# Tracing the RWKV branch's bonus sum behind the DeltaNet branch's second projection, and down's first split two steps earlier

## Chip, core and metric

One core of a Trainium2 chip runs the whole layer as one program. The metric is the device time of one execution in microseconds (us), the median of several runs. The engines are called by their names and by those in the profile: TensorE (PE; its weight loads are PEld), Vector (DVE), Scalar (ACT), GpSimd (POOL), and SyncE (SP), whose queue issues nearly all transfers.

## The reference, cut to what matters

A decoder layer on 1040 tokens (16 meta tokens and 1024) of width 1024, all in float32: a half-step SwiGLU network, a mixer of two branches A and B, a second SwiGLU network.

```python
h = h + 0.5 * swiglu(rmsnorm(h, g1), w_gu1, w_down1)     # hidden width 2816
u = rmsnorm(h, gm)
aq, ak, av, az, abeta, aalpha, bcols, ga, gb = split(u @ w_in)
# A: causal conv of 4 taps on q, k, v, then silu; q, k to unit length; chunked gated DeltaNet
# B: r, k, v from bcols (token shift); RWKV-7 scan gives y, group norm, then
y = y + sum(r * k * r_k, axis=head) * v                  # the bonus
h = h + (sigmoid(ga) * o_a + sigmoid(gb) * o_b) @ w_out
h = h + 0.5 * swiglu(rmsnorm(h, g2), w_gu2, w_down2)
out = rmsnorm(h, gf)[meta tokens dropped]
```

## The kernel before, in words

**Precision.** Every large product is made of parts in a fast matmul format. `split` (L155) writes a rounded copy `hi` with Scalar and the remainder `lo` with Vector; for weights and activations in `mm3` (L255) each 128-row step takes three matmuls: weights hi by input hi, weights hi by input lo, weights lo by input hi. So the third matmul of a projection is the first to read the weights' remainder.

**The networks.** `ffn1` and `ffn2` compute gate and up products in units (`gate_up`, L435), store the hidden tiles to DRAM, and `down` (L606) loads them back, splits each (`Hidden.put`, L577) and multiplies. A generator `Hidden.ahead` (L582) is stepped inside the last two units of `gate_up`: its first step issues the loads of the first three hidden tiles, later steps fetch and split two weight tiles, and one step splits hidden tile 0 into a tile of its own (`hd0`).

**The mixer.** `middle` (L802) runs 16 iterations: 8 pairs of heads for a first token segment of 528 columns (16 meta and 512), then the same 8 for the second segment of 512. The order of the parts within an iteration is written out in strings (L183 to L188); the regular one is "merge_blocks transitions operands+ inverses+ chains gates finish decay++ new_b++ new_a++", where each + is an iteration ahead. Two parts matter here, always one after the other:

- `new_b` (L1138) projects B's v, k and r for the iteration two ahead (`shifted` calls `proj`, which is 24 matmuls of 512 columns in the second segment, 48 of half that width in the first), normalizes k into kkn with a column sum over TensorE (`colsum_rsqrt`, L1041), and forms the inputs of the scan on Vector. Its last lines (L1181 to L1186) are the bonus: Vector makes bv = r * r_k * k, Scalar and Vector split it into the pair `hl`, TensorE sums it over each head's 64 rows with two matmuls into the bank `bon`, and Vector multiplies by v. The product is read by `finish` (L1640) two iterations later.
- `new_a` (L1189) does A's k, q and v in this order: projection, evacuation by Scalar into xr and acc, three taps of the conv on Vector (L1209), a silu on Scalar, and for k and q a column sum for the length (`cs`, `ones`).

`hl` is one pair for all column sums (`parts_tile`, L1035, one buffer). v, k, r, kkn, xr and acc are tiles of the tag `tmp`, eight slots, each of which is handed on when its last reader is done.

**What sets the order of the work.** The code only traces the instructions. When the kernel is built, a planner that works with its own costs for each instruction fills each engine's queue: of the instructions that it takes to be ready, the one traced earliest goes first; one traced later may go ahead while an earlier one isn't ready. The queues so made are fixed, and on the chip each engine takes its own in that order. In the trace, `bon`'s two matmuls have others between and around them that were traced later. Moving code in the trace order thus moves a rank, not a place.

**Weights.** `loadw` (L228) keeps one weight tile fetched ahead: when a projection is traced, the next one's transfer and split are traced with it. Two buffers hold the split weights.

Of the kernel before, what the change touches and what calls it, by code (L numbers as in the profile page):

```python
# [9 lines left out]
F32R = mybir.dt.float32r  # L10
AF = mybir.ActivationFunctionType
ALU = mybir.AluOpType
# [14 lines left out]
FULL = 512  # L27
# [127 lines left out]
def split(g, src, hi, lo, eng=None, hi_eng=None):  # L155
    if hi_eng:
        hi_eng.tensor_copy(hi, src)
    else:
        g.nc.scalar.activation(hi, src, AF.Copy)  # L159
    (eng or g.nc.vector).tensor_tensor(lo, src, hi.bitcast(F32), op=ALU.subtract)  # L160
# [55 lines left out]
def fetchw(g):  # L216
    if not g.worder[g.wfetched]:
        del g.worder[g.wfetched]
    name, idx, kk = g.worder[g.wfetched]
    g.wfetched += 1  # L220
    raw = g.wp.tile([P, KD, P], F32, name="wraw", tag="wraw", bufs=2)
    g.nc.sync.dma_start(raw[:, :kk, :], g.a[name][idx])
    w = g.wp.tile([P, 2, KD, P], F32R, name="w", tag="w", bufs=WB)
    split(g, raw[:, :kk, :], w[:, 0, :kk, :], w[:, 1, :kk, :])
    g.wready.append((name, idx, w))


def loadw(g, name, *idx):  # L228

    while g.wfetched < min(g.wused + 1 + AHEAD, len(g.worder)) and g.worder[g.wfetched]:  # L230
        fetchw(g)
    g.wused += 1
    n, i, w = g.wready.pop(0)
    assert (n, i) == (name, idx)
    return w
# [12 lines left out]
def mm_tile(g, name, n=512, first=256):  # L248

    t = g.mm.tile([P, 512 * g.mmw], F32, name=name, tag="mm")  # L250
    o = 512 - first if n > 512 else 0
    return t[:, o : o + n]


def mm3(g, ps, w, kk, rhs):  # L255
    n = 3 * kk
    i = 0
    for k in range(kk):
        hi, lo = rhs(k)
        for l, r in ((w[:, 0, k, :], hi), (w[:, 0, k, :], lo), (w[:, 1, k, :], hi)):  # L260
            g.nc.tensor.matmul(ps, lhsT=l, rhs=r, start=i == 0, stop=i == n - 1)  # L261
            i += 1
# [298 lines left out]
class Hidden:  # L561
# [20 lines left out]
    def ahead(self):  # L582
        for f in range(self.AHEAD):
            self.load(f)
        yield
        yield
        fetchw(self.g)
        yield
        self.first = self.put(self.tile(self.pool, F32R, "hd0", "hd0", 1, [2]))
        yield  # L590
        yield
        fetchw(self.g)
        yield
# [274 lines left out]
def tmp_tile(g, name, w=528):  # L868
    return g.st.tile([P, w], F32, name=name, tag="tmp", bufs=NTMP)
# [54 lines left out]
def proj(g, c, ct, full=False):  # L924

    w = loadw(g, "win", ct)
    lo, n = (c.off, FULL) if full else (0, c.n)
    ps = mm_tile(g, "pp", n, FULL // 2 + c.off)
    for c0, cn in halves(n, FULL // 2 + c.off):
        sl = slice(lo + c0, lo + c0 + cn)  # L930
        mm3(g, ps[:, c0 : c0 + cn], w, KD, lambda k: (c.u[k][:, 0, sl], c.u[k][:, 1, sl]))
    return ps
# [92 lines left out]
def halves(n, first=256):  # L1025
    return [(0, first), (first, n - first)] if n > 512 else [(0, n)]
# [111 lines left out]
def new_b(g, q):  # L1138

    nc, st, V, c, j, n, off, it = g.nc, g.st, g.V, q.c, q.j, q.n, q.off, q.it  # L1140
    meta = q.s == 0
    fs = slice(off, off + FULL)
    tmp = lambda name, w=528: tmp_tile(g, name, w)
    EN, ELx, av, elm = q.EN, q.ELx, q.av, meta and q.elm

    v = shifted(g, c, 48 + j, 16 + j, "vB")


    Vs = q.Vs = st.tile([P, NCB, CB], F32, name="Vs", tag="Vs", bufs=2)
    k = shifted(g, c, 40 + j, 8 + j, "kB")  # L1150
    for ps, cs in run(g, g.mx, "vbp", lambda i, h: (v[HS[h], off + i * CB : off + (i + 1) * CB],
                                                    g.C("cmat")[HS[h], HS[h]], h, key(i, h)))[0]:
        nc.scalar.activation(Vs[:, cs], ps, AF.Copy)
    if meta:
        ps = g.mx.tile([P, 512], F32, name="vbm", tag="mx")
        nc.tensor.matmul(ps[:16, 0:P], lhsT=v[:, 0:16], rhs=g.C("cmat"), start=True, stop=True)
        nc.scalar.activation(g.uvm[it % 2][0:16, :], ps[:16, 0:P], AF.Copy)

    r = shifted(g, c, 32 + j, j, "rB")
    kkn = tmp("kkn")  # L1160
    colsum_rsqrt(g, "bd", k[:, :n], kkn, kkn, n, 1.0, V("eps"), pre=V("kk", j))
    nc.vector.scalar_tensor_tensor(kkn[:, :n], k[:, :n], V("kk", j), kkn[:, :n], op0=ALU.mult, op1=ALU.mult)
    t1 = tmp("t1")
    nc.vector.tensor_tensor(t1[:, :n], av[:, :n], kkn[:, :n], op=ALU.mult)
    nc.scalar.activation(av[:, :n], av[:, :n], AF.Identity, scale=V("ka", j), bias=V("oka", j))
    nc.vector.tensor_tensor(k[:, :n], k[:, :n], av[:, :n], op=ALU.mult)
    BK = q.BK = st.tile([P, NCB, 2, CB], F32, name="BK", tag="BK")
    nc.vector.tensor_tensor(BK[:, :, 1, :], ch3(k[:, fs], CB), ch3(EN[:, fs], CB), op=ALU.mult)
    nc.vector.scalar_tensor_tensor(BK[:, :, 0, :], ch3(t1[:, fs], CB), -1.0, ch3(EN[:, fs], CB),
                                   op0=ALU.mult, op1=ALU.mult)  # L1170
    AR = q.AR = st.tile([P, NCB, 2, CB], F32, name="AR", tag="AR", bufs=2)
    nc.vector.tensor_tensor(AR[:, :, 0, :], ch3(kkn[:, fs], CB), ELx[:, :, 0:CB], op=ALU.mult)
    if meta:
        arm = q.arm = st.tile([P, 16], F32, name="arm", tag="arm", bufs=2)
        nc.vector.tensor_tensor(arm, kkn[:, 0:16], elm[:, 0:16], op=ALU.mult)
        nc.vector.tensor_tensor(g.bkm[:, 0:16], k[:, 0:16], EN[:, 0:16], op=ALU.mult)
        nc.vector.scalar_tensor_tensor(g.bkm[:, 32:48], t1[:, 0:16], -1.0, EN[:, 0:16], op0=ALU.mult, op1=ALU.mult)

    nc.vector.tensor_tensor(AR[:, :, 1, :], ch3(r[:, fs], CB), ELx[:, :, 1:], op=ALU.mult)
    bv = q.bv = st.tile([P, FULL], F32, name="bv", tag="bv", bufs=2)  # L1180
    nc.vector.scalar_tensor_tensor(bv, r[:, fs], V("rk", j), k[:, fs], op0=ALU.mult, op1=ALU.mult)  # L1181
    ps = g.mx.tile([P, 512], F32, name="bon", tag="mx")
    hi, lo = parts_tile(g, FULL)
    split(g, bv, hi, lo)
    colsum(g, ps, "bd", hi, lo)
    nc.vector.tensor_tensor(bv, ps, v[:, fs], op=ALU.mult)  # L1186


def new_a(g, q):  # L1189

    nc, st, V, c, j, n, off = g.nc, g.st, g.V, q.c, q.j, q.n, q.off
    meta = q.s == 0
    tmp = lambda name, w=528: tmp_tile(g, name, w)
    kq = q.kq = st.tile([P, 2, 528], F32, name="kq", tag="kq", bufs=2)
    for wi, base in ((0, 8), (1, 0), (2, 16)):
        ct = base + j
        ps = proj(g, c, ct)
        xr = tmp("xr", 531)
        acc = tmp("acc")
        if c.s == 0:  # L1200
            nc.gpsimd.memset(xr[:, 0:3], 0.0)
        else:
            nc.gpsimd.tensor_copy(xr[:, 0:3], g.carA[:, ct, :])
        nc.scalar.activation(xr[:, 3 : 3 + n], ps, AF.Copy)
        nc.scalar.activation(acc[:, :n], ps, AF.Identity, scale=V("convw", ct * 4 + 3))  # L1205
        if c.s == 0:
            nc.gpsimd.tensor_copy(g.carA[:, ct, :], xr[:, n : n + 3])
        for tap in (2, 1, 0):
            nc.vector.scalar_tensor_tensor(acc[:, :n], xr[:, tap : tap + n], V("convw", ct * 4 + tap), acc[:, :n],  # L1209
                                           op0=ALU.mult, op1=ALU.add)  # L1210
        sg = xr
        sigm(nc, sg[:, :n], acc[:, :n], scale=-1.0)
        nc.vector.tensor_tensor(acc[:, :n], acc[:, :n], sg[:, :n], op=ALU.mult)
        if wi < 2:
            colsum_rsqrt(g, "ones", acc[:, :n], sg, sg, n, 1.0, V("eps"),
                         bias=V("lnq") if wi == 1 else None)
            nc.vector.tensor_tensor(kq[:, wi, :n], acc[:, :n], sg[:, :n], op=ALU.mult)
    Va = q.Va = st.tile([P, NCA, P], F32, name="Va", tag="Va", bufs=2)
    ps = g.mx.tile([P, 512], F32, name="vap", tag="mx")
    for i in range(NCA):  # L1220
        nc.tensor.transpose(ps[:, i * P : (i + 1) * P], acc[:, off + i * CA : off + (i + 1) * CA], g.C("ident"))
    nc.scalar.activation(Va, ch3(ps, P), AF.Copy)
    if meta:
        vkm = q.vkm = st.tile([16, 2, P], F32, name="vkm", tag="vkm", bufs=2)
        ps = g.mx.tile([P, 512], F32, name="vmp", tag="mx")
        nc.tensor.matmul(ps[:16, 0:P], lhsT=acc[:, 0:16], rhs=g.C("ident"), start=True, stop=True)
        nc.scalar.activation(vkm[:, 0, :], ps[:16, 0:P], AF.Copy)
# [510 lines left out]
```

## Time and profile before

| | |
|---|---|
| median of 3 runs | 3052.4 us (3052.31 to 3053.04) |
| the profiled execution | 3048.16 us |
| its span, first to last instruction | 3046.4 us |
| TensorE busy | 2942.3 us, 97% |
| Vector busy | 2007.7 us, 66% |
| Scalar busy | 1372.2 us, 45% |
| GpSimd busy | 348.6 us, 11% |
| mean granted clock of TensorE, share of full | 0.993 |

The span is that of the one execution whose trace was taken; its own time is 1.8 us longer, and the median of the runs 4.2 us above that. A timeline row reads: start, duration, engine, source line, operation, output <- inputs by tile names, shape, count of merged instructions, and in brackets the idle time of that engine just before, with what released it. The first network runs to about 732 us; the last column sum of the mixer is at 2301.7 us, and the second network follows the output projection, from 2364 us on.

### The profile page before, as it was taken

What the parts mean: (1) busy time and instruction counts of PE and PEld (TensorE: products, weight loads), DVE (VectorE), ACT (ScalarE), POOL (GpSimd) and SP (SyncE); (2) the same over time, 40 slices, a digit from 0 to 9 for tenths busy, and PEclk for the clock granted to TensorE, in tenths of its full rate; (3) what the DMA queues carried; (4) which work ended last, traced back from release to release, by engine and by line L of the source; (5) the groups of instructions that cost most, each with busy time, mean ns of one, the idle gap of its engine ahead of it and who ended that gap; (6) DMA issues with size and microseconds to landing.
All of it is one profiled execution on the core that took longest, in us unless ns stands there. A gap on an engine that the chain in (4) does not pass through costs nothing.

```text
span 3046.4 us, 61663 instructions
## 1 busy us (share of the span) xinstructions
PE 2942.3 (97%) x25498; PEld 2530.1 (83%) x25498; DVE 2007.7 (66%) x3872; ACT 1372.2 (45%) x2404; POOL 348.6 (11%) x503
## 2 busy tenths in 40 slices
PE   8999999999989999999998999999999999999998
PEld 8999998998878888888776777777786888888886
DVE  7555554346668877778868888777766755556246
ACT  5322222125645656556565655665544432223114
POOL 0322220000000000000000110010000032232000
PEclk9999999999999999999999999999999999999999
DMA  3232224234222322233332333223345132225223
GB/s 127 83 98 84 83 82 160 81 94 149 80 67 72 78 74 67 78 82 97 82 92 67 91 80 81 74 74 88 106 145 178 64 104 90 83 83 202 58 80 115
DMA packets 257593, 287.19 MB, mean 94 GB/s; under 512 B 169296, under 2 KB 175440, under 8 KB 257312
## 3 DMA queue, kind: packets, MB, share of 16 engines
q1 hardware_dynamic: 253072, 271.43, 30.2%
q0 software_dynamic: 2512, 8.65, 0.8%
q8 instruction: 201, 3.29, 0.5%
q10 hardware_dynamic: 1728, 3.16, 0.3%
q14 instruction: 80, 0.66, 0.1%
HBM read 232.70 MB, written 50.47 MB: 93 GB/s over the span
## 4 chain that ended last, share of the span: by engine, by line
PE 52%; DVE 10%; ACT 5%; issue 2%; DMA 1%; SPq 0%; DVEq 0%; ACTq 0%
PE pp L261 16%; PE pg L448 13%; PE pd L261 8%; PE pwo L261 3%; PE pg L472 1%; DVE w L160 1%; DVE tb L1400 1%; DVE Xb L1402 1%; ACT w L159 1%; PE vp L1085 1%; PE cs L1032 1%; PE mp L1085 1%; PE np L1085 1%; DVE mt L1508 1%; PE bkt L1317 1%
## 5 line engine op out<-in xcount | busy, mean ns | idle before, releaser
L261 PE MATMUL pp<-uk,w 128*128 128x512 f32 (+2 forms) x4824 | 966.6, 346 | 9.3 <-DVE w L160 5.7
L261 PEld LDWEIGHTS pp<-uk,w 128*128 128x128 f32 x4824 | 741.3, 190 | 105.5 <-DVE w L160 13.2
L159 ACT ACTIVATE w<-wraw 128x1024 fp32r<-128x1024 f32 (+2 forms) x330 | 326.4, 989 | 497.5 <-PE pd L261 301.7
L261 PE MATMUL pd<-hd,w 128*128 128x512 f32 (+2 forms) x2448 | 454.4, 346 | 5.3 <-ACT hd L159 3.1
L160 DVE TENSOR_TENSOR w<-wraw,w 128x1024 fp32r<-128x1024 f32 (+2 forms) x330 | 403.2, 1222 | 74.8 <-ACT w L159 64.9
L261 PEld LDWEIGHTS pd<-hd,w 128*128 128x128 f32 x2448 | 391.8, 189 | 63.9 <-ACT hd L159 3.3
L448 PE MATMUL pg<-bt,w 128*128 128x256 f32 (+2 forms) x2520 | 400.7, 317 | 0.0
L448 PEld LDWEIGHTS pg<-bt,w 128*128 128x128 f32 x2520 | 360.4, 188 | 32.8
L454 DVE TENSOR_TENSOR c<-c,pg 128x520 f32<-128x520 f32 (+1 forms) x280 | 189.6, 689 | 278.3 <-PE pg L448 250.6
L448 PE MATMUL pg<-b,w 128*128 128x256 f32 (+2 forms) x2160 | 347.8, 317 | 0.0
L448 PEld LDWEIGHTS pg<-b,w 128*128 128x128 f32 x2160 | 309.8, 188 | 28.0
L159 ACT ACTIVATE w<-wrx 128x1024 fp32r<-128x1024 f32 (+1 forms) x64 | 58.4, 913 | 289.8 <-PE pg L448 247.9
L418 POOL TENSOR_TENSOR wrx<-wrx 128x512 f32<-128x512 f32 x38 | 52.5, 1382 | 732.8 <-DVE w22b L160 519.0
L1402 DVE TENSOR_TENSOR Xb<-Xb,tb 115x126 f32<-115x126 f32 (+22 forms) x496 | 125.4, 253 | 9.1 <-DVE tb L1400 0.4
L1400 DVE TENSOR_TENSOR tb<-Ub,Xb 115x126 f32<-115x126 f32 (+22 forms) x496 | 124.1, 250 | 8.1 <-DMA Ub<-scr 0.9
L1209 DVE SCALAR_TENSOR_TENSOR acc<-xr,pk,acc 128x528 f32<-128x528 f32 (+1 forms) x144 | 108.8, 756 | 28.6 <-ACT acc L1205 28.0
L624 DVE SCALAR_TENSOR_TENSOR h<-pd,h 128x528 f32<-128x528 f32 (+1 forms) x64 | 44.6, 698 | 116.4 <-PE pd L261 116.4
L624 DVE SCALAR_TENSOR_TENSOR hh<-pd,hh 128x512 f32<-128x512 f32 x64 | 44.1, 690 | 115.2 <-PE pd L261 115.2
L261 PE MATMUL pwo<-uk,w 128*128 128x512 f32 x384 | 99.7, 413 | 4.1 <-DVE w L160 1.9
L261 PEld LDWEIGHTS pwo<-uk,w 128*128 128x128 f32 x384 | 73.8, 197 | 21.9 <-ACT w L159 2.7
L160 DVE TENSOR_TENSOR w<-wrx,w 128x1024 fp32r<-128x1024 f32 (+1 forms) x64 | 66.6, 1041 | 14.9 <-ACT w L159 14.8
L159 ACT ACTIVATE hd<-hr 128x1040 fp32r<-128x1040 f32 (+1 forms) x40 | 41.2, 1061 | 63.3 <-DMA hr<-hid 38.3
(420 smaller groups left out, 4200.4 us busy)
## 6 DMA issues: line engine op xcount, KB each, us to landing
wraw<-in_win SPq DMA_DIRECT2D x150, 512.0 KB
wraw<-in_wgu SPq DMA_DIRECT2D x44, 512.0 KB
wrx<-in_wgu SPq DMA_DIRECT2D x44, 512.0 KB
wraw<-in_wdn SPq DMA_DIRECT2D x48, 320.0 KB
wraw<-in_wdn SPq DMA_DIRECT2D x32, 384.0 KB
hid<-c SPq DMA_DIRECT2D x44, 260.0 KB
hr<-hid SPq DMA_DIRECT2D x22, 520.0 KB
hid<-c SPq DMA_DIRECT2D x44, 256.0 KB
```

The lines of the kernel that those rows point to most:

```text
L159: g.nc.scalar.activation(hi, src, AF.Copy)
L160: (eng or g.nc.vector).tensor_tensor(lo, src, hi.bitcast(F32), op=ALU.subtract)
L261: g.nc.tensor.matmul(ps, lhsT=l, rhs=r, start=i == 0, stop=i == n - 1)
L418: sums.tensor_tensor(a22, a21, a22, op=ALU.add)
L448: nc.tensor.matmul(ps[:, c0 : c0 + cn], lhsT=l[:, x, k, :], rhs=r[:, k, y, c0 : c0 + cn], start=i == 0, stop=i == 3 * HK - 1)
L454: nc.vector.tensor_tensor(o, x, y, op=ALU.add)
L472: nc.tensor.matmul(ps[:, c0 : c0 + cn], lhsT=l[:, x, k, :], rhs=r[:, k, y, c0 : c0 + cn], start=i == 0, stop=i == 6 * HK - 1)
L624: nc.vector.scalar_tensor_tensor(hv, pd, 0.5, hv, op0=ALU.mult, op1=ALU.add)
L1085: g.nc.tensor.matmul(ps[e][HS[dst], c0 : c0 + CB], lhsT=l, rhs=r, start=True, stop=True)
L1209: nc.vector.scalar_tensor_tensor(acc[:, :n], xr[:, tap : tap + n], V("convw", ct * 4 + tap), acc[:, :n], op0=ALU.mult, op1=ALU.add)
L1400: nc.vector.tensor_tensor(tv, U[:, i, i + 1 :].unsqueeze(2).to_broadcast([npt, nt, ncc]), X[:, i, 0:ncc].unsqueeze(1).to_broadcast([npt, n ...
L1402: nc.vector.tensor_tensor(X[:, i + 1 :, 0:ncc], X[:, i + 1 :, 0:ncc], tv, op=ALU.add)
```

## The change

The bonus loses its place at the end of `new_b`: its last five lines after bv (the split, the two matmuls and the product with v) become a function `bonus`, which `new_a` calls after tracing the projection of q (its second, `wi == 1`), ahead of q's evacuation. bv itself stays in `new_b`. In `Hidden.ahead`, which both networks use, the split of hidden tile 0 is traced at the generator's second step instead of its fourth.

```diff
--- before.py
+++ after.py
@@ -583,10 +583,10 @@
         for f in range(self.AHEAD):
             self.load(f)
         yield
+        self.first = self.put(self.tile(self.pool, F32R, "hd0", "hd0", 1, [2]))
         yield
         fetchw(self.g)
         yield
-        self.first = self.put(self.tile(self.pool, F32R, "hd0", "hd0", 1, [2]))
         yield
         yield
         fetchw(self.g)
@@ -1179,11 +1179,16 @@
     nc.vector.tensor_tensor(AR[:, :, 1, :], ch3(r[:, fs], CB), ELx[:, :, 1:], op=ALU.mult)
     bv = q.bv = st.tile([P, FULL], F32, name="bv", tag="bv", bufs=2)
     nc.vector.scalar_tensor_tensor(bv, r[:, fs], V("rk", j), k[:, fs], op0=ALU.mult, op1=ALU.mult)
+    q.v = v
+
+
+def bonus(g, q):
+
     ps = g.mx.tile([P, 512], F32, name="bon", tag="mx")
     hi, lo = parts_tile(g, FULL)
-    split(g, bv, hi, lo)
+    split(g, q.bv, hi, lo)
     colsum(g, ps, "bd", hi, lo)
-    nc.vector.tensor_tensor(bv, ps, v[:, fs], op=ALU.mult)
+    g.nc.vector.tensor_tensor(q.bv, ps, q.v[:, q.off : q.off + FULL], op=ALU.mult)
 
 
 def new_a(g, q):
@@ -1195,6 +1200,8 @@
     for wi, base in ((0, 8), (1, 0), (2, 16)):
         ct = base + j
         ps = proj(g, c, ct)
+        if wi == 1:
+            bonus(g, q)
         xr = tmp("xr", 531)
         acc = tmp("acc")
         if c.s == 0:
```

## Rows read from the trace of the kernel before

**Rows 1.** Page, part 1: busy us, share of the span, instructions.
```profile
PE 2942.3 (97%) x25498; PEld 2530.1 (83%) x25498; DVE 2007.7 (66%) x3872; ACT 1372.2 (45%) x2404; POOL 348.6 (11%) x503
```

**Rows 2.** TensorE's waits, whole span: us in total, times, longest.
```profile
PE bon L1032 <- ACT hl L159: 17.8, 13, 7.6
PE np L1085 <- DVE AR L1511: 9.0, 14, 1.0
```

**Rows 3.** TensorE timeline, bon: start, us, [idle before, releaser].
```profile
783.01 0.50 PE L1032 MATMUL bon<-hl,bdr 128*128 128x512 f32 x1 [0.41 <-ACT hl L159]
...
1631.86 0.79 PE L1032 MATMUL bon<-hl,bdr 128*128 128x512 f32 x1 [7.60 <-ACT hl L159]
...
1722.85 0.50 PE L1032 MATMUL bon<-hl,bdr 128*128 128x512 f32 x1 [1.47 <-ACT hl L159]
...
1896.61 0.50 PE L1032 MATMUL bon<-hl,bdr 128*128 128x512 f32 x1 [1.49 <-ACT hl L159]
...
2157.41 0.50 PE L1032 MATMUL bon<-hl,bdr 128*128 128x512 f32 x1 [1.31 <-ACT hl L159]
```

**Rows 4.** TensorE timeline around bon, in both halves.
```profile
1147.45 0.52 PE L1032 MATMUL cs<-hl,onesr 128*128 128x256 f32 x2
...
1886.31 8.80 PE L261 MATMUL pp<-uk,w 128*128 128x512 f32 x38
...
1896.95 1.79 PE L261 MATMUL pp<-uk,w 128*128 128x512 f32 x7
...
1906.82 0.39 PE L1032 MATMUL cs<-hl,onesr 128*128 128x512 f32 x1
...
1910.95 0.39 PE L1032 MATMUL cs<-hl,onesr 128*128 128x512 f32 x1
```

**Rows 5.** Scalar timeline: the writes of hl.
```profile
1146.77 0.63 ACT L1046 ACTIVATE hl<-acc 128x528 fp32r<-128x528 f32 x1
...
1895.92 0.63 ACT L159 ACTIVATE hl<-bv 128x512 fp32r<-128x512 f32 x1 [0.69 <-DVE bv L1181]
...
1905.48 0.61 ACT L1046 ACTIVATE hl<-acc 128x512 fp32r<-128x512 f32 x1
...
1910.15 0.63 ACT L1046 ACTIVATE hl<-acc 128x512 fp32r<-128x512 f32 x1
```

**Rows 6.** Vector timeline around bv and the taps (acc).
```profile
1144.80 0.77 DVE L1209 SCALAR_TENSOR_TENSOR acc<-xr,pk,acc 128x528 f32<-128x528 f32 x1 [2.09 <-ACT acc L1205]
...
1896.47 1.22 DVE L160 TENSOR_TENSOR w<-wraw,w 128x1024 fp32r<-128x1024 f32 x1
1897.60 0.78 DVE L160 TENSOR_TENSOR hl<-bv,hl 128x512 fp32r<-128x512 f32 x1
1898.30 0.77 DVE L1209 SCALAR_TENSOR_TENSOR acc<-xr,pk,acc 128x512 f32<-128x512 f32 x1
1899.00 0.69 DVE L1186 TENSOR_TENSOR bv<-bon,vB 128x512 f32<-128x512 f32 x1
...
1900.98 1.54 DVE L1209 SCALAR_TENSOR_TENSOR acc<-xr,pk,acc 128x512 f32<-128x512 f32 x2 [0.62 <-ACT acc L1205]
```

**Rows 7.** TensorE timeline around the wait of 7.60 us.
```profile
1623.53 0.74 PE L261 MATMUL pp<-uk,w 128*128 128x512 f32 x2 [0.42 <-ACT w L159]
...
1632.48 1.22 PE L261 MATMUL pp<-uk,w 128*128 128x512 f32 x2
```

**Rows 8.** Vector timeline there: the weights' remainder.
```profile
1631.22 1.22 DVE L160 TENSOR_TENSOR w<-wraw,w 128x1024 fp32r<-128x1024 f32 x1
```

**Rows 9.** Scalar timeline: down's first split in each network.
```profile
77.73 1.08 ACT L159 ACTIVATE hd<-hr 128x1040 fp32r<-128x1040 f32 x1
...
2411.86 1.05 ACT L159 ACTIVATE hd<-hr 128x1024 fp32r<-128x1024 f32 x1
```

**Rows 10.** TensorE timeline at the head of down, both networks.
```profile
483.75 0.86 PE L261 MATMUL pd<-hd,w 128*128 128x256 f32 x4 [3.10 <-ACT hd L159]
...
2788.52 0.84 PE L261 MATMUL pd<-hd,w 128*128 128x512 f32 x3
```

## The prediction

> **What bounds the kernel now.** I read the page's busy shares first. TensorE is busy 97% of the span, 2942.3 of 3046.4 us, so 104.1 us are left that any reordering could win; Vector has 66%, Scalar 45% [rows 1]. Then the list of what TensorE waited for, longest first. At its head stands the matmul that the change moves: the bonus sum `bon`, held 17.8 us in 13 waits, each time released by Scalar's write of `hl`; `np` (9.0 us in 14 waits) is among the next [rows 2]. Then the timeline of TensorE, for where the 13 waits lie: one of 7.60 us at 1631.86, six in the last six iterations, from 1.47 to 1.31 us (8.75 us together), and six in the first half, the largest 0.41 us, which leaves 17.8 - 7.60 - 8.75 = 1.5 us [rows 3]. So what can be won at once is small: 17.8 us is 0.58%, and a measurement of this kernel tells about 0.2%, 6.1 us, from no change.
>
> One iteration shows the mechanism. Behind the column sum of kkn come 38 projection matmuls, 24 of A's k and 14 of A's q; then `bon` stands in the queue and waits 1.49 us, with ten matmuls of q behind it that lacked nothing [rows 3, 4]. Scalar wrote `hl` at 1895.92 as soon as Vector had made bv [rows 5]. The place of `bon` in the queue was fixed when the kernel was built, so the plan expected bv about 1.5 us sooner than Vector delivers it.
>
> **The change, part by part.**
>
> *The bonus sum, added and removed work:* none. Per iteration the same Scalar split, Vector remainder, two matmuls and Vector product are issued, no DMA, no bank and no tile more. Only their rank moves: behind the projections of k and q and behind k's Vector and Scalar work.
>
> *TensorE.* `bon` can now come only behind q's 24th matmul. In the iteration shown that is ten matmuls later; seven took 1.79 us, so ten take about 2.3 us, more than the 1.49 us wait [rows 3, 4]. `hl` was complete at 1895.92 + 0.63 = 1896.55; q, no longer stopped at 1896.61 - 1.49 = 1895.12, would end near 1897.4, so the six waits of 8.75 us go at `bon` itself [rows 5].
>
> *Where a part comes back.* The next matmul that needs the same late Vector chain is the column sum of k: its `hl` was ready at 1905.48 + 0.61 = 1906.09, and TensorE arrived at 1906.82, 0.73 us late [rows 4, 5]. A TensorE that arrives 1.49 us sooner waits 1.49 - 0.73 = 0.76 us there, if the sum keeps its distance to k's chain. It may not: Vector's remainder (0.78 us) and product (0.69 us) leave the places between k's taps, so k's chain itself runs up to 1.47 us sooner [rows 6]; the plan will use this to place the sum earlier (then 0.76 us comes back), or leave it where it is (then nothing does). No row decides between these ends, so I take the middle, 0.38 us. Gain per iteration: 8.75/6 - 0.38 = 1.08 us, over six iterations 6.5 us; the ends are 6 x 0.70 = 4.2 and 8.75 us.
>
> *First half.* The 1.5 us of waits there are followed by a column sum of k with 1147.45 - (1146.77 + 0.63) = 0.05 us of slack, so I count them as returned: 0 (ends 0 and 1.5) [rows 4, 5].
>
> *The long wait.* The 7.60 us at 1631.86 look like the prize, and I give 0 for them. Just before, TensorE ran only two matmuls of q, and behind `bon` two more at 1632.48 [rows 3, 7]. A projection's third matmul is its first to read the weights' remainder. Vector wrote that remainder from 1631.22 to 1632.44, and TensorE's next projection matmul starts at 1632.48, 0.04 us behind it [rows 7, 8]. With `bon` gone from there, q's third matmul waits for Vector until 1632.44 all the same. Vector's work up to that point does not change.
>
> *Vector and Scalar.* The two Vector instructions, 1.47 us, now stand behind k's taps and ahead of q's. In the first half Vector sat idle 2.09 us before a tap of q, which hides them; in the second half 0.62 us, which hides less than half [rows 6]. What remains delays q's chain by up to 0.85 us; its column sum has 1910.95 - (1910.15 + 0.63) = 0.17 us of slack [rows 4, 5]. But q's projection also ends sooner, so I count 0 and keep the loss for the last rival. Scalar has nothing else to run at 1895.92 and can keep its split there; the split then holds the only `hl` pair until the second `bon` matmul, near 1900, and k's column sum asks for it at 1905.48: covered by 5 us [rows 5]. The tile of v is held some 2 us longer, until the product; it is one of eight `tmp` slots. The remainder of v's weights ends at 1896.47 + 1.22 = 1897.69, and v's third matmul comes some three matmuls (`bon` and two of v, 0.26 us each) after 1897.4, near 1898.1: 0.4 us of cover, the next thing that would be late [rows 6].
>
> *The split of down's first input.* It is traced earlier, but it already runs far earlier than either place: at 77.73 us in the first network and 2411.86 in the second, over 370 us before the head of down in either [rows 9, 10]. Its load and its tile were free then and no later rank held it back, so a higher rank changes nothing: 0. The wait of 3.10 us at the head of down is for a later input's split, which the change leaves alone [rows 10]. Bounds: at best those 3.1 us, at worst one split that is pushed in front of work, 1.06 us. The SP queue's order of loads does not change with it.
>
> **Sum:** 0 + 0 - 6.5 + 0 = -6.5 us. Against the profiled execution (3048.16 us, span 3046.4) that gives 3041.7; its median of runs is 3052.4, 4.2 us above that execution, so I forecast 3052.4 - 6.5 = 3045.9 us.
>
> **The rivals.**
>
> *More comes out.* The six waits go whole (8.75), with the first half's 1.5: 10.2 us, 3042.2. If the new order also moves the weights' remainder ahead in the long wait, 17.8 us go: 3034.6. For it: k's chain is relieved by 1.47 us. Against it: slacks of 0.05 and 0.17 us at the next sums, and Vector full in the long wait. Chance 0.20.
>
> *All comes back.* TensorE's lead of 1.1 us per iteration is taken at the sums of k and q and at `np`, which already waits up to 1.0 us [rows 2]. Then 3052.4. For it: the small slacks. Against it: these chains begin at TensorE's own matmuls and move forward with it. Chance 0.12.
>
> *The repeating gap is a shortage of storage, not of data.* Then `bon` would wait for its bank or its `hl` pair wherever it stands, and the time stays at 3052.4. Against it: every row names Scalar's write of `hl` as the releaser, and that write waited for bv alone [rows 2, 5]. Chance 0.04. The Trainium skill (Perfetto Trace Analysis, section Identifying Performance Opportunities, at its strategy) says of such "consistent bubbles" that they "can mean there isn't enough SBUF/PSUM for the next tile to be allocated". The rows here point to data instead; by that rule the sum would be 0.
>
> *Slower.* The remainder and the product, 1.47 us, stand in front of q's taps in all 16 iterations, and TensorE pays for them at q's column sum. Price: 16 x (1.47 - 0.17) = 20.8 us, less the 10.2 us won: +10.6, 3063.0. It decides once Vector's idle time before q's taps is below 1.47 us in both halves; in the second it is 0.62, in the first 2.09 [rows 6]. That cover shrinks if Scalar's evacuation of q comes sooner. Chance 0.18.
>
> **How the numbers follow.** The forecast has 0.46; its own range, 3043.6 to 3048.2, lies across the bound of 0.2% at 3046.3, so half counts as faster and half as the same. Faster: 0.23 + 0.20 = 0.43. Same: 0.23 + 0.12 + 0.04 = 0.39. Slower: 0.18. The range goes from 3039 (the larger gain without the long wait, 3042.2, less the 3.1 us at down's head) to 3060 (most of the slower case's way); that leaves out the gain of 17.8 us and the slower case at its full price, about 0.2.
>
> **What would show it.** Right: the `bon` waits of about 1.5 us are gone, `bon` stands directly behind q's 24th matmul, a wait of 0 to 0.8 us appears at k's column sum, the long wait stays but is put down to the weights' remainder, and down's first split runs at its old times. Wrong: a long wait that is really gone, a column sum of q that waits over 0.5 us per iteration, or a changed order in either network.

## The result, and the profile after

The changed kernel takes 3056.79 us (median of 18 runs) where the kernel before, beside it, takes 3052.32 (18 runs): ratio 1.0017, 95% interval 1.0011 to 1.0024. It is slower by some 5 us. The forecast was 6.5 us faster.

The page of the changed kernel, part 1, answers to [rows 1]:

```profile
PE 2947.1 (96%) x25498; PEld 2546.6 (83%) x25498; DVE 2010.5 (66%) x3872; ACT 1372.8 (45%) x2404; POOL 324.0 (11%) x503
```

No instruction came or went on these engines, yet TensorE is 4.8 us busier [rows 1]: the same matmuls took longer. Its waits, whole span (us in total, times, longest), answer to [rows 2]:

```profile
PE pp L261 <- DVE w L160: 16.1, 7, 8.2
PE iv L1466 <- ACT T L1463: 9.7, 5, 1.9
...
PE cs L1032 <- ACT hl L1046: 7.8, 9, 2.8
PE np L1085 <- DVE AR L1518: 7.8, 15, 1.0
```

`bon`, with 17.8 us the head of the old list, is gone from it. A new wait stands there: `iv` of line 1466, the fourth product of `merge_blocks`, five times 1.9 us.

Where the time went is read from one instruction that occurs once per iteration, Scalar's exponential of kkn (L1053). Its 11th and 16th, in the kernel before:

```profile
1714.43 0.63 ACT L1053 ACTIVATE kkn<-kkn 128x512 f32<-128x512 f32 x1
...
2149.36 0.63 ACT L1053 ACTIVATE kkn<-kkn 128x512 f32<-128x512 f32 x1
```

and in the changed one:

```profile
1717.66 0.63 ACT L1053 ACTIVATE kkn<-kkn 128x512 f32<-128x512 f32 x1
...
2164.41 0.63 ACT L1053 ACTIVATE kkn<-kkn 128x512 f32<-128x512 f32 x1
```

Five iterations take 434.93 us before, 86.99 each, and 446.75 after, 89.35 each: +11.8 us. By the same marker the first half changed by 0.8 (770.6 and 771.4 us for eight iterations), the two iterations at the switch to the second half lost 2.0, and from the last marker to the second network 4.1 came back (214.4 and 210.3); the networks are unchanged. With 0.4 at the start that is 10.9 us, the difference of the two spans. The profiled execution of the kernel before lay 4.2 us under its median and that of the changed kernel 2.4 us above, so the medians differ by less, 4.5 us. The small parts are those of one execution each: in e1 below, which is the same plan, the switch lost 0.9 and 2.2 came back. This mean of five iterations is the figure that the experiments below are compared by, beside their times.

TensorE's timeline in the changed kernel: first, from an earlier iteration, what stands behind the long wait, then one of the five iterations:

```profile
1633.35 7.22 PE L261 MATMUL pp<-uk,w 128*128 128x512 f32 x19 [8.23 <-DVE w L160]
...
1894.58 16.50 PE L261 MATMUL pp<-uk,w 128*128 128x512 f32 x72
...
1912.55 0.39 PE L1032 MATMUL cs<-hl,onesr 128*128 128x512 f32 x1
...
1915.32 0.40 PE L1032 MATMUL bon<-hl,bdr 128*128 128x512 f32 x1
...
1918.92 0.50 PE L1032 MATMUL cs<-hl,onesr 128*128 128x512 f32 x1
...
1921.52 0.76 PE L1461 MATMUL iv<-XA,UA 64*64 64x64 f32 x8
1924.21 0.50 PE L1466 MATMUL iv<-Y,T 64*64 64x64 f32 x5 [1.93 <-ACT T L1463]
...
1925.59 1.04 PE L1228 MATMUL vap<-ck,acc 128*128 128x128 f32 x4
```

Scalar's timeline of the same stretch:

```profile
1911.40 0.61 ACT L1046 ACTIVATE hl<-acc 128x512 fp32r<-128x512 f32 x1
...
1914.25 0.62 ACT L159 ACTIVATE hl<-bv 128x512 fp32r<-128x512 f32 x1
...
1918.07 0.61 ACT L1046 ACTIVATE hl<-acc 128x512 fp32r<-128x512 f32 x1
...
1922.52 0.72 ACT L1055 ACTIVATE xr<-xr,pk 128x512 f32<-128x512 f32 x1
1923.13 0.62 ACT L955 ACTIVATE xr<-xr 128x512 f32<-128x512 f32 x1
1923.78 0.38 ACT L1463 ACTIVATE T<-iv 64x256 f32<-64x256 f32 x1
```

The pair `hl` goes to k's column sum first (1911.40), then to the bonus (1914.25), then to q's (1918.07). So `bon` stands not behind q's 24th projection matmul but behind k's column sum, with all of k's, q's and v's projections (the 72 matmuls from 1894.58) done. q's length is made that much later, and its last exponential (1922.52) and a step of v's silu now run on Scalar ahead of the copy that `merge_blocks` needs (1923.78). In the kernel before, the same product of merge waited for nothing:

```profile
1917.61 0.56 PE L1454 MATMUL iv<-XA,UA 64*64 64x64 f32 x5
...
1918.85 0.50 PE L1459 MATMUL iv<-Y,T 64*64 64x64 f32 x5
```

Behind this wait the clock falls. Stretches of the changed kernel (start to end, length, busy us of PE, PEld, DVE, ACT, POOL, granted clock, DMA share, GB/s):

```profile
1915.00:1922.00 7.00, 7.00 (x84) 4.98 (x83) 6.69 (x13) 6.10 (x11) 0.00 (x0) 1.00 0.01 2
1922.00:1925.80 3.80, 1.87 (x47) 1.63 (x45) 3.10 (x7) 3.75 (x9) 0.00 (x0) 0.99 0.25 61
1925.80:1929.30 3.50, 3.50 (x57) 3.09 (x56) 0.88 (x2) 3.04 (x10) 0.19 (x1) 0.52 0.23 88
```

So 3.5 us at half clock cost about 1.7 us more. Four of the five waits brought such a fall, one of them of 6.8 us; behind the wait that ends at 1745.45, which is as long, the clock stayed up:

```profile
1745.40:1748.90 3.50, 3.45 (x92) 3.06 (x92) 1.13 (x3) 3.45 (x10) 0.19 (x1) 1.00 0.51 154
```

That is some 17 us at half clock over the five iterations, or 1.7 us lost in each on the mean. Against the 1.49 us that `bon` no longer waits stand 1.93 us of new wait and 1.7 us of slow clock: 2.1 us of the 2.36 by which the iteration is longer.

### The profile page after: what moved, and what is told of

It is laid out like the page before. It is cut to its first block, busy times and chain, and to the rows that moved or that the text cites. A ratio compares the mean times of both kernels' runs of the same rounds, so it can differ in the third digit from the quotient of the medians.

```text
span 3057.3 us, 61667 instructions
## 1 busy us (share of the span) xinstructions
PE 2947.1 (96%) x25498; PEld 2546.6 (83%) x25498; DVE 2010.5 (66%) x3872; ACT 1372.8 (45%) x2404; POOL 324.0 (11%) x503
## 4 chain that ended last, share of the span: by engine, by line
PE 77%; DVE 12%; ACT 6%; issue 2%; DMA 2%; DVEq 0%; SPq 0%; ACTq 0%
PE pg L448 25%; PE pp L261 18%; PE pd L261 16%; PE pg L472 3%; PE pwo L261 2%; DVE w L160 1%; DVE Xb L1409 1%; DVE tb L1407 1%; PE vp L1085 1%; PE xp L1085 1%; PE cs L1032 1%; ACT w L159 1%; PE mp L1085 1%; DVE mt L1515 1%; PE bkt L1324 1%
```

## The experiments

All times are medians beside runs of the kernel before on the same chip; the ratio is to that kernel. "Iteration" is the mean of the five iterations above, one profiled execution each.

| run | us | before | ratio (95%) | iteration |
|---|---|---|---|---|
| before | | | | 86.99 |
| changed | 3056.79 | 3052.32 | 1.0017 (1.0011 to 1.0024) | 89.35 |
| e1 bonus part alone | 3057.84 | 3050.79 | 1.0021 (1.0011 to 1.0032) | 89.49 |
| e3 changed, copy on Vector | 3052.61 | 3050.79 | 1.0004 (0.9995 to 1.0012) | 87.35 |
| e5 changed, own pair | 3078.20 | 3050.79 | 1.0091 (1.0077 to 1.0104) | 91.91 |
| e8 own pair, split as before | 3074.98 | 3050.79 | 1.0080 (1.0068 to 1.0093) | 92.21 |
| f3 before, bon behind q's 24th, 2nd half | 3074.36 | 3051.50 | 1.0082 (1.0070 to 1.0095) | 92.23 |
| f1 the same, both halves | 3080.62 | 3051.50 | 1.0098 (1.0084 to 1.0112) | 92.42 |
| f2 behind q's 18th, 2nd half | 3051.69 | 3051.50 | 1.0004 (0.9995 to 1.0013) | 87.16 |
| e4 before, copy on Vector | 3043.79 | 3051.50 | 0.9975 (0.9966 to 0.9985) | 86.95 |
| g1 f3 with k's weights early | 3049.75 | 3051.17 | 1.0002 (0.9993 to 1.0010) | 87.05 |
| g5 before, k's weights early | 3050.86 | 3051.17 | 1.0003 (0.9995 to 1.0012) | 87.09 |
| g4 g5 with copy on Vector | 3044.21 | 3051.17 | 0.9978 (0.9969 to 0.9987) | 87.21 |
| g2 g1 with copy on Vector | 3043.94 | 3051.17 | 0.9974 (0.9964 to 0.9983) | 86.85 |
| h1 before, copy late by order | 3044.92 | 3052.05 | 0.9976 (0.9965 to 0.9988) | 85.42 |
| h3 changed, copy two places ahead | 3047.92 | 3052.05 | 0.9985 (0.9976 to 0.9994) | 87.21 |
| h2 g5 without the bonus, 2nd half | 3044.68 | 3052.05 | 0.9972 (0.9960 to 0.9983) | 86.66 |
| i1 changed, copy late by order | 3075.60 | 3050.85 | 1.0085 (1.0072 to 1.0099) | 91.55 |
| i2 g1 with copy late by order | 3034.33 | 3050.85 | 0.9945 (0.9933 to 0.9957) | 84.38 |
| j1 i1 with k's weights early | 3056.99 | 3052.26 | 1.0016 (1.0006 to 1.0025) | 88.70 |

**The two parts apart.** e1 puts down's first split back:

```diff
-        self.first = self.put(self.tile(self.pool, F32R, "hd0", "hd0", 1, [2]))
         yield
         fetchw(self.g)
         yield
+        self.first = self.put(self.tile(self.pool, F32R, "hd0", "hd0", 1, [2]))
```

> The changed kernel with the first edit undone: down's first split runs where it ran in the kernel before, the bonus part stands as changed. Theory A (the loss sits in the second half's iterations alone, in the new wait of the fourth merge product for Scalar's copy): the time is the changed kernel's, 3054 to 3059 us, and the long 8.2 us wait of the one iteration stays. Rival (the early split is what loses, through the storage or the Scalar time that it takes): the time goes back to 3051 to 3053 us or below.

It is the changed kernel. The early split does nothing; in the changed kernel it runs at 77.97 and 2422.84 us, as far ahead of its use as in [rows 9, 10].

**The copy.** e3 moves merge's copy to Vector in the changed kernel, e4 in the kernel before:

```diff
-    nc.scalar.activation(T64[64:128], ch3(ps3[64:128, 0:256], 64), AF.Copy)
+    nc.vector.tensor_copy(T64[64:128], ch3(ps3[64:128, 0:256], 64))
```

> The changed kernel with one edit: the copy of the second 64-row half of merge_blocks' product goes to Vector instead of Scalar, so that it no longer stands behind the logarithm and exponentials of A's chains. Theory A (the new 1.93 us wait of the fourth merge product in each of the six iterations of the second half, and the half clock that follows it for some 3.4 us each, are the whole loss): that wait falls below 0.5 us, the granted clock is back at 0.99 to 1.00 in the second half, and the time falls by 6 x (1.4 to 3.2) us, to 3037 to 3049 us. Rival B (the clock falls for another reason, the two bonus products in another place): the wait goes, the clock stays at 0.96 to 0.98, and the time falls by 6 x 1.5 = 9 us at most, to 3046 to 3050 us. Rival C (the place of the split itself loses): 3054 to 3060 us, with the idle time of TensorE turned up at another product.

> The control of the run with merge's copy on Vector: the same one edit on the kernel before, where the fourth merge product waits for nothing. Theory A (in the changed kernel that edit cured a wait, it is no gain by itself): the time is the kernel before's within 3 us. Rival (the move of the copy is worth several us in either kernel): 5 us or more below the kernel before, and then what it gave back in the changed kernel says little on the new wait.

In e3 the wait of merge's fourth product falls to 0.57 us, the iteration is back at 87.35 and its clock at 1.00, much as theory A has it; but the time lies outside the ranges of all three theories, since behind the last marker 4.6 to 6.5 us were lost again (216.8 us to the second network; 212.2 in e1 and 210.3 in the changed kernel). And e4, the control, gained 7.6 us in the kernel before, outside these iterations (86.95). So e3's time alone proves nothing. h3 keeps the copy on Scalar and takes it ahead of q's last exponential in the changed kernel by an order edge (NOSYNC stands for a dependency that only orders two instructions of one engine):

```diff
-        nc.scalar.activation(out[:, :n], out[:, :n], AF.Exp, scale=-0.5, bias=bias)
+        g.qexp = nc.scalar.activation(out[:, :n], out[:, :n], AF.Exp, scale=-0.5, bias=bias)
...
-    nc.scalar.activation(T64[64:128], ch3(ps3[64:128, 0:256], 64), AF.Copy)
+    t64 = nc.scalar.activation(T64[64:128], ch3(ps3[64:128, 0:256], 64), AF.Copy)
+    if q.s == 1 and q.it < 2 * NJ - 1:
+        g.tc.add_manual_dep(g.qexp.ins, t64.ins.name, NOSYNC, reason="order")
```

> The changed kernel with one order edge in the second half: the last exponential of q's length goes behind merge's copy on Scalar, which so moves two instructions ahead and stays on its engine. Theory A: the 1.93 us wait of the fourth merge product falls below 0.8 us, the granted clock is back at 0.99 to 1.00, each iteration is 1 to 2.5 us shorter, and the time is 6 to 14 us below the changed kernel, at or below the kernel before. Rival (the loss lies in another place of the changed order, as in q's late chain itself): the wait falls, and the time stays within 3 us of the changed kernel.

The wait falls to 0.81 us, the clock is 1.00, the iteration 87.21, and the time is below the kernel before by 0.15%, some 4.6 us. That settles it for the change as it stands: 2.14 of the 2.36 us that it lost in each of these iterations are this copy, two instructions too late on Scalar, with the clock behind it. One iteration of h3 (columns as above) shows the clock:

```profile
1826.00:1913.00 87.00, 84.50 (x941) 68.74 (x940) 70.18 (x167) 52.36 (x102) 6.53 (x15) 1.00 0.31 82
```

**The pair of its own.** Was the shared pair what put `bon` behind k's column sum?

```diff
-    hi, lo = parts_tile(g, FULL)
+    hi, lo = q.bp = [g.st.tile([P, FULL], F32R, name=n, tag=t) for n, t in (("bh", "xa"), ("bl", "xv"))]
```

> The changed kernel with one edit: the bonus value's two parts have storage of their own (the tags of xa and xv) and no longer share the one pair of k's and q's column sums. Theory D (the shared pair is what put the split behind k's column sum, and so the two bonus products behind all of A's projections and Scalar's copy of the merge late): the bonus products stand directly behind q's 24th projection product as forecast, the wait of the fourth merge product is below 0.5 us, and the time is 3042 to 3050 us. Rival (its rank in the order, not the storage, sets its place): the products stay behind the projections and the time stays at 3054 to 3060 us.

e8 has the same pair, with the split left in new_b:

```diff
     q.v = v
+    q.bp = [st.tile([P, FULL], F32R, name=n, tag=t) for n, t in (("bh", "xa"), ("bl", "xv"))]
+    split(g, bv, *q.bp)
...
-    hi, lo = parts_tile(g, FULL)
-    split(g, q.bv, hi, lo)
+    hi, lo = q.bp
```

> The bonus value's two parts have storage of their own and are made where the kernel before makes them, in new_b; only the column sum and the product with v stand behind A's second projection. This is the order that the forecast took for granted. Theory A with D: no wait of the bonus products, no wait of the fourth merge product, the time of the forecast, 3043 to 3049 us. Rival (the product with v on Vector between q's and v's chains delays these chains by itself): a wait of 1 us or more at q's or v's column sum, or at the merge, in each iteration, and 3052 us or more.

In both, `bon` still stands behind all projections and behind the first matmul of k's column sum. TensorE of e5:

```profile
1901.80 16.50 PE L261 MATMUL pp<-uk,w 128*128 128x512 f32 x72
...
1919.76 0.40 PE L1032 MATMUL cs<-hl,onesr 128*128 128x512 f32 x1
1920.00 0.40 PE L1032 MATMUL bon<-bh,bdr 128*128 128x512 f32 x1
```

though its own pair was complete on Vector over 7 us sooner:

```profile
1911.97 0.69 DVE L160 TENSOR_TENSOR bl<-bv,bh 128x512 fp32r<-128x512 f32 x1
```

So the shared pair delays the split in the changed kernel, but it is not what places the two matmuls: theory D falls there. Its second part came true: the wait of merge's fourth product is 0.42 us in both runs. They lost 24 to 28 us all the same, at another product: B's k projection waits 1.94 to 1.97 us for Scalar's part of its weights in each of the five iterations, as in f3 below. The Trainium skill (Perfetto Trace Analysis, section Identifying Performance Opportunities) says that a gap that repeats can mean a lack of storage. The pair of its own (in two tags that exist already) did not make these runs faster; but with that new loss in them they do not tell what storage alone is worth; h1 below, which adds no storage, tells more of this gap.

**The forecast's own place.** An order edge on the kernel before keeps `bon` behind q's 24th matmul and leaves everything else as traced:

```diff
+            if i == 24 - 1:
+                g.mark = g.last
...
         ps = proj(g, c, ct)
+        if wi == 1 and c.s == 1:
+            for m in q.bon:
+                g.tc.add_manual_dep(m.ins, g.mark.ins.name, NOSYNC, reason="order")
```

`g.last` is the projection matmul just traced and `q.bon` the two bonus matmuls. f1 has `wi == 1` alone, for both halves; f2 marks `18 - 1`.

> The kernel before with one thing added: in the second half an order edge, without data, that keeps the two bonus products behind q's 24th projection product. Split, storage, rank and all else stay as in the kernel before, so this is the place that the forecast named. Theory A (the forecast's mechanism is right and only the place was not reached by the change): the bonus products' six waits are gone, 0 to 0.8 us comes back at k's column sum, no wait at the fourth merge product, the granted clock stays at 1.00, and the time is 4 to 9 us below the kernel before. Rival (what is won at the bonus sum comes back at the next waits of the iteration, as at the merge and at np): within 3 us of the kernel before, with waits of about 1.5 us more per iteration at other products. Rival C (the place itself brings the loss): 3 us or more above it.

> The same edge in both halves. In the first half q's projection has 48 products of half the width, so the bonus products come some 5 us later than in the kernel before and hold the one pair until then. Theory A: the first half's waits at the bonus sum, 1.5 us, are returned at k's column sum, and the time is that of the run with the edge in the second half alone, within 2 us. Rival (the pair, held longer, delays k's column sum): k's column sum waits 0.5 to 2 us in each of the first half's iterations, 3 to 12 us more than the run with the edge in the second half alone.

> The edge behind q's 18th product, second half alone: four matmuls later than in the kernel before, about 1.0 us, where the wait was 1.49. Theory A: the six waits fall to about 0.5 us each and the time is 3 to 6 us below the kernel before, between that kernel and the run with the 24th. Rival (all comes back at the next waits): within 3 us of the kernel before.

f3 on TensorE: `bon` is where the forecast had it and waits for nothing, and 65 us on, B's k projection waits for its weights.

```profile
1910.35 0.62 PE L1033 MATMUL bon<-hl,bdr 128*128 128x512 f32 x2
...
1975.40 0.73 PE L261 MATMUL pp<-uk,w 128*128 128x512 f32 x2 [1.96 <-ACT w L159]
1976.92 0.73 PE L261 MATMUL pp<-uk,w 128*128 128x512 f32 x2 [0.79 <-ACT w L159]
1978.64 1.65 PE L261 MATMUL pp<-uk,w 128*128 128x512 f32 x3 [0.99 <-DVE w L160]
```

On Scalar the split of these weights starts 9.3 us behind the gate's evacuation, with 16 instructions in between, all but two of them of finish and decay:

```profile
1965.00 0.60 ACT L956 ACTIVATE gg<-pp 128x512 f32<-128x512 f32 x1 [1.43 <-PE pp L261]
1965.49 0.62 ACT L1047 ACTIVATE AR<-yb 128x512 f32<-128x512 f32 x1
...
1974.30 1.04 ACT L159 ACTIVATE w<-wraw 128x1024 fp32r<-128x1024 f32 x1
```

In the kernel before it follows directly, 0.5 us from start to start:

```profile
1952.91 0.60 ACT L954 ACTIVATE gg<-pp 128x512 f32<-128x512 f32 x1 [1.21 <-PE pp L261]
1953.41 1.05 ACT L159 ACTIVATE w<-wraw 128x1024 fp32r<-128x1024 f32 x1
```

The split is traced with v's projection, later than finish and decay. By the planner's rule it goes ahead of them only where they are not ready at that moment, and one moved column sum upset that; g1 below tests this. f1 loses 6.3 us more, in the first half and within its rival's range; k's column sum waits there in five iterations, 0.16 to 0.90 us, which is 2.6 us of it. f2 loses and wins nothing: its bonus waits became two per iteration, for Scalar's half of the pair and for Vector's.

**The weights' split in time.** g1 is f3 with k's weights fetched at the end of gates; g5 is the control; g4 and g2 add e3's copy to g5 and g1.

```diff
     nc.vector.tensor_tensor(gg, ps, gg, op=ALU.mult)
+    if c.s == 1 and q.it + 2 < 2 * NJ:
+        fetchw(g)
```

> The run with the edge behind q's 24th product in the second half, with one thing more: the weights of B's k are fetched at the end of gates, one projection earlier in the trace, so that their split ranks ahead of the instructions of finish and decay on Scalar. Theory E (the place behind q's 24th is harmless; the 23 us were lost because the plan then put that split behind some 15 Scalar instructions, 8 to 9 us late, and k's projection waited for it): the waits for Scalar's write of the weights, 1.96 and 0.79 us per iteration, are gone, and the time is 20 us or more below the run with the edge alone, 3 to 9 us below the kernel before. Rival (the place itself costs, through the chains behind it): the weights' wait goes and other waits of the same sum take its place; 10 us or more above the kernel before.

> The control: the same earlier fetch on the kernel before alone, where that split already stands directly behind the gate's evacuation. Theory E: nothing to gain, within 3 us of the kernel before. Rival (the earlier fetch is a gain by itself): 5 us or more below it.

> The kernel before with merge's copy on Vector and with the earlier fetch. If both only mend what the other plans broke, the time is that of the kernel before with the copy on Vector, 6 to 9 us below the kernel before; if they add up, 10 us or more below it.

> The edge behind q's 24th product, the earlier fetch and merge's copy on Vector together: the forecast's place with both known losses taken away. Theory E: the six bonus waits are gone on top of the copy's gain, so 10 to 16 us below the kernel before. Rival (what is won at the bonus sum comes back at the next waits): the same as the kernel before with the copy on Vector, 6 to 9 us below the kernel before.

g1 wins back f3's whole loss, 24.6 us between the two medians, and g5 shows that the fetch is worth nothing by itself: theory E holds for the loss. But g1 ends at the kernel before, not 3 to 9 us below it. TensorE of g1:

```profile
1902.36 0.39 PE L1033 MATMUL bon<-hl,bdr 128*128 128x512 f32 x1
1903.66 0.50 PE L1033 MATMUL bon<-hl,bdr 128*128 128x512 f32 x1 [0.91 <-DVE hl L160]
...
1910.08 0.49 PE L1033 MATMUL cs<-hl,onesr 128*128 128x512 f32 x1 [0.45 <-ACT hl L1048]
...
1924.78 0.50 PE L1464 MATMUL iv<-Y,T 64*64 64x64 f32 x5 [0.31 <-ACT T L1461]
```

0.91 + 0.45 + 0.31 = 1.67 us: the 1.49 us is back within the iteration. Over the six iterations these three products wait 7.6 us, where `bon` had waited 8.75. g2 equals e4 and g4, so the place won nothing there either.

**A late copy, known to the order.** h1 puts the copy behind z's silu in the kernel before; i1 does it in the changed kernel, i2 in g1, j1 is i1 with g1's fetch. `q.t64` is the copy, and `sigm` (the silu's helper) returns its last instruction here.

```diff
-    sigm(nc, zg, pz, scale=-1.0)
+    last = sigm(nc, zg, pz, scale=-1.0)
+    if q.s == 1 and hasattr(q, "t64"):
+        g.tc.add_manual_dep(q.t64.ins, last.ins.name, NOSYNC, reason="order")
```

> The kernel before with one order edge in the second half: merge's copy of the second 64-row half stays on Scalar but goes behind the three instructions of z's silu, some 2.4 us later than it ran. Theory A (a late copy is what the changed kernel pays for): the fourth merge product waits about 2 us per iteration, the granted clock falls to 0.96 to 0.98 in these iterations, each is 2 to 3 us longer, and the time is 8 to 20 us above the kernel before. Rival (that wait is covered by the other waits of the iteration): the wait appears, other waits shrink by as much, and the time stays within 4 us of the kernel before.

> The changed kernel with the order edge that puts merge's copy, still on Scalar, behind the three instructions of z's silu: later than in the changed kernel, but known when the order is made. Theory G (a late copy costs only where TensorE's queue has nothing put in front of the product that needs it): operands' products stand between the third and the fourth merge product, that wait is below 0.8 us, and the time is 7 to 15 us below the changed kernel. Rival (a late copy costs as such): the wait stays at 1.9 us or grows, and the time is the changed kernel's or above.

> The kernel before with that edge for the copy, the bonus products behind q's 24th product and the earlier fetch of k's weights. If the forecast's place is worth its 6.5 us once nothing else in the order is hurt, the time is 10 to 15 us below the kernel before; if the place is worth nothing, it is that of the run with the copy's edge alone, 5 to 9 us below the kernel before.

> The changed kernel with the later copy and with k's weights fetched one projection earlier in the second half. Theories E and G together (the changed kernel's own mechanism is sound once the copy is late by plan and the split is in time): no wait of 1.9 us for Scalar's weights or at the merge, a granted clock of 1.00, and 8 to 16 us below the kernel before. Rival (bonus products behind k's column sum cost by themselves, as they do not stand at the forecast's place): no more than 4 us below the kernel before, or above it.

h1 went against what I expected: 7 us faster, the iteration 85.42. Its TensorE:

```profile
1894.58 0.50 PE L1032 MATMUL bon<-hl,bdr 128*128 128x512 f32 x1 [0.28 <-ACT hl L159]
...
1915.72 0.56 PE L1454 MATMUL iv<-XA,UA 64*64 64x64 f32 x5
...
1916.32 1.47 PE L1247 MATMUL grb<-AR,BK 64*64 64x128 f32 x37
...
1918.87 0.50 PE L1459 MATMUL iv<-Y,T 64*64 64x64 f32 x5 [0.46 <-ACT T L1456]
```

From merge's third product to its fourth there are 3.15 us instead of 1.24, and 46 of operands' products lie between them where the kernel before has 16. The copy itself ran 2.7 us behind the third product, and TensorE waited 0.46 us for it, where it waits 1.93 in the changed kernel. And `bon`, which h1 does not move, waits only 0.28 us here, 0.34 on the mean of the five iterations: Vector starts on bv 7.8 us behind the last matmul of kkn's column sum, where it is 9.05 in the kernel before. This shorter wait is 1.15 of the 1.57 us that the iteration gained. Why the new plan reaches bv sooner stays open.

i2 is the best run of all: 16.8 us below the kernel before, more than either of its expectations, iteration 84.38, and `bon` behind q's 24th without a wait. Its TensorE:

```profile
1894.91 0.62 PE L1033 MATMUL bon<-hl,bdr 128*128 128x512 f32 x2
...
1916.32 0.50 PE L1464 MATMUL iv<-Y,T 64*64 64x64 f32 x5 [0.46 <-ACT T L1461]
```

From h1 to i2 the iteration falls by 1.04 us. That this is near the forecast's 1.08 is luck: in h1 `bon` waits 0.34 us, so its new place can have taken away no more than that. Of the 1.04 us, 0.24 is idle time of TensorE; 0.80 is busy time of the same 4702 matmuls at a granted clock of 1.00 (417.18 us over the five iterations in h1, 413.18 in i2), which no run explains. i2 also has the earlier fetch; h1 with the fetch alone, or with the place alone, was not run. So i2 shows what the three edits win together and not what the forecast's place is worth.

i1 has merge's wait at 0.49 to 0.66 us in four of six iterations and at 1.11 in two, much as theory G said, but it loses 25 us to the kernel before: projections wait up to 1.95 us for their weights again. j1 mends that and is back at the changed kernel's time, not below: now a projection behind merge's third product waits for Vector's part of its weights.

```profile
1912.76 0.40 PE L1032 MATMUL bon<-hl,bdr 128*128 128x512 f32 x1
...
1921.07 1.66 PE L261 MATMUL pp<-uk,w 128*128 128x512 f32 x6 [1.35 <-DVE w L160]
```

i2 and j1 carry the same two additions and differ in the bonus part, the place of `bon` and the ranks of its split and product (and in down's split, which e1 found to be worth nothing): 84.38 against 88.70 us per iteration. With both additions the changed kernel's bonus part is the dearer one; place and ranks were not tested apart.

**Without the bonus.** h2 is g5 with the bonus sum left out in the second half:

```diff
-    ps = g.mx.tile([P, 512], F32, name="bon", tag="mx")
+    if c.s == 0:
+        ps = g.mx.tile([P, 512], F32, name="bon", tag="mx")
...
```

> The kernel before with the earlier fetch of k's weights, and without the bonus sum in the second half: its split, its two products and the product with v are left out there (bv stays, unsummed). This takes away the six waits of 1.49 us, two products of 0.26 us, 1.47 us of Vector and 0.63 us of Scalar per iteration, with no place for the wait to come back at the bonus sum. Theory F (another bound sets the iteration's length, so the wait at the bonus sum is slack that appears elsewhere): 0 to 4 us below the kernel before. Rival (TensorE's own queue sets it): 6 x (1.49 + 0.5) = 12 us or more below, and then a right place for the sum would have won most of 8.75 us.

8.5 us by the ratio, between theory F and its rival. The iteration is 86.66, only 0.43 below g5's, though 1.49 us of waiting and two matmuls are gone: within these iterations other waits took the place, as theory F has it. But what bounds them belongs to the plan and is no bound of the work: h1 and i2 do the whole of it in 85.42 and 84.38. Leaving the whole sum out won less than the three edits of i2 did with the sum in place.

## Why the prediction was wrong

*The place, the step that failed.* "`bon` can now come only behind q's 24th matmul", and I took it to come there. It came behind k's column sum, 84 projection matmuls behind kkn's sum instead of 48. The kernel's description ahead of it says that moved code moves a rank and not a place; the prediction then used the rank as one. The step beside it, "the split then holds the only `hl` pair ... covered by 5 us", assumed the bonus would take the pair first; k's sum, traced ahead, took it, and Scalar did not "keep its split there" but made it at 1914.25. What came of this order is Scalar's late copy for merge, a cost that the sum had at 0: 1.93 us of waiting and 1.7 of slow clock per iteration, more than the 1.49 us won. Why the matmuls stand there even with a pair of their own stays open. One candidate was not tested: `bon` and the column sums of new_b and new_a also take their banks from one tag (`mx`). In the second half's regular iterations of all twenty traces the matmuls reach the banks of this tag in the order in which they are traced, and the change traces `bon` behind k's sum. A bank of its own for `bon` would decide it.

*The six waits go* (8.75 us): right, they went. *A part comes back at k's column sum*, 0 to 0.76 us per iteration: mis-sized and at the wrong matmul. In the changed kernel the new wait is at merge's fourth product, in five iterations. Even at the forecast's place (g1) 1.67 us came back in the iteration shown, and 7.6 of the 8.75 us over all six. About half of that was in the trace: the prediction called the pair complete at 1896.55, when only Scalar's half was. Vector's remainder ends later, behind that of the weights, and the second matmul reads it: 0.91 us.

*The first half*, 0: right within 1 us, but not as argued. The waits did move from `bon` to k's column sum and grew there, to 0.65 to 1.37 us in five iterations; that the half is only 0.8 us longer for it no row explains. *The long wait*, 0: right, and for the reason given. With `bon` gone it is 8.23 us, released by Vector's weights' remainder. *Down's first split*, 0: right (e1).

*The rivals.* "All comes back" describes g1; "more comes out" describes no run of the bonus's place alone. "A shortage of storage" found no support: in h1, with no storage added, the gap shrinks from 1.49 to 0.34 us as bv comes sooner. So it was late data, as the prediction read it. "Slower" named q's taps on Vector, in all 16 iterations. The loss was on Scalar, in the second half only, and smaller than its 10.6 us. No rival had the rest of the order change, and in the experiments such changes took runs from 17 us below the kernel before to 30 above.

## What to carry to other kernels

Where a planner makes the queues, a moved rank is a new plan: read which storage and which place the moved part gets, and look for what now stands behind it on the helper engines, before pricing the wait that it had. The wait that recurred in each iteration here meant that the plan and the chip disagreed on when bv is ready. An order edge, or tracing a late step earlier, tells the plan; try these together, since alone the edge for `bon` lost 23 us, the earlier fetch won nothing and the edge for the copy won 7, and together they won 16.8. And when a run hits the forecast's figure, look whether the wait it was to remove was still there.

## What the runs showed of the hardware

In the changed kernel an idle gap of 1.93 us in five iterations brought, in four of them, 3.4 to 6.8 us at the lower clock level (0.50 to 0.52 granted, 1.2 GHz); in the iteration shown TensorE was 49% busy in the 3.8 us around the gap. Four `vap` transposes took 1.04 us at the lower level and 0.66 in the kernel before. Behind the fifth gap, at 1745.45, the clock stayed at 1.00, and in e1 too one of the five gaps, another one, brought no fall. The 1.49 us gap of `bon` in the kernel before was followed by a clock of 1.00 throughout. f3's three gaps in a row, 3.74 us in all, brought a stretch at the lower level that began in the third:

```profile
1978.40:1981.70 3.30, 3.06 (x7) 2.48 (x8) 3.24 (x10) 0.00 (x0) 0.00 (x0) 0.50 0.67 207
```

So a gap's price is not its length alone: a wait moved from one place to another may bring the lower clock, and the same gap does not bring it every time.
